# Feed-forward products accumulated in one PSUM bank, activation sums formed with the gate and streamed through DRAM

## The chip, the cores and the metric

The kernel runs on one core of one Trainium2 chip. Its time is the device time of one execution in microseconds (us). Five engines work side by side, each in the order of its own instructions: PE (TensorE, matrix products; its weight loads, PEld, overlap them), DVE (VectorE), ACT (ScalarE), POOL (GpSimd) and SP (which here only issues transfers). They meet through semaphores. DMA engines move data between DRAM and the on-chip memory SBUF. PE writes its products to PSUM, eight banks of 128 x 512 float32 values; DVE and ACT read them there, POOL does not.

## The reference

The program is one layer of a network on 1024 rows of 1024 float32 values: three mixers, a merge with a projection, and a feed-forward. Only the feed-forward is changed:

```python
gu = rms_norm(x, g_ffn[l]) @ w_ffn_in[l]          # 1024 x 1024 by 1024 x 5632
g_, u_ = jnp.split(gu, 2, axis=-1)
x = x + (jax.nn.silu(g_) * u_) @ w_ffn_out[l]     # 1024 x 2816 by 2816 x 1024
```

## The kernel before

**Numbers.** Every float32 operand of a product is split into a high part, which ACT writes (line 105), and a low part, which DVE forms by subtraction (line 106). A product of two split operands is three matmuls (`mm3`, lines 121 to 123): high by high, low by high, high by low. A tile named `fwh` or `foh` is a high part, `fwl` or `fol` a low part.

**Seven products.** Each large product is cut into 2 x 2 blocks and done by the seven block products of Winograd's scheme in place of eight. The operands of the seven are sums of blocks, and the results are sums of products.

**First product.** The width of 5632 columns is worked on in 22 blocks: block j has the same 128 columns of gate and of value (`g_`, `u_`) for all 1024 rows. The tokens' side is kept in SBUF, split, in seven versions: the quarters "11", "21", "22" and the sums "T1" to "T4" (tiles `hh`, `hl`). For each block, `ffn_first` loads half of the block's weights and makes the products with "11" and "21"; `ffn_rest` loads the other half, lets POOL form four weight sums (lines 1153 to 1156), splits them, and makes the five other products. One product (`prod`) is 12 matmuls of 128 x 512 into one bank; banks are taken in turn, eight of them. Each product is read from its bank at once and added into SBUF by DVE (lines 1144, 1162 to 1168). Then comes the gate, by a Tanh on ACT and two operations of DVE for each half of the rows (lines 1180 to 1182); it leaves out a factor of 0.5, which is made up for when the last product is added to x. Activations go to DRAM (`act_dram`), but for those of the last pair of blocks, which stay. `ffn_first` runs two blocks ahead of `ffn_rest`.

**Last product.** The width of 2816 is worked on in 11 pieces of 2 x 128 (`kk`). The sum over the pieces stays in PSUM: two sets of four banks, one bank for each 128 rows of a half of the tokens. There are four steps (`plan`), each over all pieces, with two products a piece, the last with one; a product is four groups of three matmuls. For each piece the step's function (`prep1` to `prep4`) loads weights and activations, forms the sums of either (POOL, marked `G`, and DVE, marked `V`, line 1241), and splits them. This runs `AHEAD = 2` pieces ahead of the products. Activations are loaded once and stay in SBUF until the end. Between steps the banks are added to `xr`, the rows of x, by DVE (line 1352), or copied by ACT and added by POOL (lines 1348 and 1349), and finished quarters are stored.

**Order of the work.** A scheduler with a model of the engines' times reorders the instructions within their dependences when the program is built; the order on each engine is then fixed. `Slots` hands out buffers of 4 KB a partition, the one that has been free longest first. Loads on SP's queue that are marked `keep_in_program_order` stay in the order of the code.

Of the kernel before, what the change touches and what calls it, by code (L numbers as in the profile page):

```python
# [30 lines left out]
AHEAD = 2  # L31
# [8 lines left out]
# Order in which the steps of the independent parts before the merge are emitted.  # L40
# [42 lines left out]
def hybrid_kernel(ctx: ExitStack, tc: tile.TileContext, x, small, cs, bias_a, lru_w, w_idx, w_zg, w_c, w_g, w_b,  # L83
# [129 lines left out]
    # The high parts of a pair of heads in their own halves of e and o, the low parts in the other halves.  # L213
# [10 lines left out]
    # Each part of a pair of heads in both halves, head by head.  # L224
# [14 lines left out]
    # q . k for 128 rows against columns k0 .. k0 + w, with q stacked and each part of k in both halves. Returns the  # L239
    # columns of the two banks.  # L240
# [114 lines left out]
    # Stacked q and k of a pair of heads from the rows of its z (q, q, k, k).  # L355
# [103 lines left out]
    # Softplus of -lambda, from exp(-|z|) by range reduction and log1p by its atanh series.  # L459
# [151 lines left out]
    # Top-k threshold of each row: its bits from the highest down, by counts.  # L611
# [5 lines left out]
    class Chain:  # L617
# [15 lines left out]
        # Go on with the first n tiles.  # L633
# [72 lines left out]
    # The high halves of the scores settle the high bits of the threshold: for these a score reaches a bound if its  # L706
    # high half does.
# [72 lines left out]
    # The sums of the quarters of hT (B11 | B12 over B21 | B22: width by tokens) that the seven products of a 2 x 2  # L780
    # block product (Winograd) take.
# [67 lines left out]
    # The products of a pair of gate columns that take quarters of hT themselves.  # L849
# [83 lines left out]
    # The projection behind the merge goes by the seven products of a 2 x 2 block product (Winograd): rows 512.. are  # L933
    # its first row block, the blocks of M (kp, kp + 2) its columns. P6 and P7 go on top of P1.
# [61 lines left out]
    hb_ = {}  # L996
# [83 lines left out]
    def bank(shape=(128, 512), at=None):  # L1080
        i = nb_[0] % 8 if at is None else at
        nb_[0] += at is None
        return psum.tile(list(shape), F32, name="B", tag=f"B{i}")

# [32 lines left out]
    fw, al, be = {}, {}, {}  # L1117
    act = {(NH - 1, h): None for h in range(2)}
    act_dram = [dram.tile([128, 2, 2, 512], F32, name=f"ad{j}") for j in range(NF // 2)]

    def split_w(raw, n):
        hi, lo = rw.get((128, n, 4, 128), F32R, "fwh"), rw.get((128, n, 4, 128), F32R, "fwl")
        split(raw, hi, lo)
        return hi, lo
# [6 lines left out]
    def prod(w, i, name):  # L1131
        p = bank()
        for k in range(4):
            hi, lo = hb_[name, k // 2]
            mm3(p, w[0][:, i, k], w[1][:, i, k], hi[:, k % 2], lo[:, k % 2], k == 0, k == 3)
        return p

    def ffn_first(j):
        load_a(j)
        al[j] = sl.get((128, 2, 512), F32, "al")  # L1140
        be[j] = sl.get((128, 2, 512), F32, "be")
# [3 lines left out]
        rw.free(*w)  # L1145

    def ffn_rest(j):
# [13 lines left out]
        x, y = al[j], be[j]  # L1161
# [7 lines left out]
        rw.free(*w12, *w34, *w22)  # L1169
        f, kk = j // NH, j % NH  # L1170
        if kk < NH - 1:
            ga = sl.get((128, 2, 512), F32, "act")
            gv = [ga[:, hf] for hf in range(2)]
        else:
            if f == 0:
                for hf in range(2):
                    act[kk, hf] = sl.get((128, 2, 512), F32, "act")
            gv = [act[kk, hf][:, f] for hf in range(2)]
        for hf, (g_, u_) in enumerate(((y[:, 0], x[:, 1]), (x[:, 0], y[:, 1]))):
            S.activation(gv[hf], g_, AF.Tanh, scale=0.5)  # L1180
            V.scalar_tensor_tensor(gv[hf], gv[hf], 1.0, g_, op0=OP.add, op1=OP.mult)
            V.tensor_mul(gv[hf], gv[hf], u_)
        sl.free(x, y)
        if kk < NH - 1:
            nc.gpsimd.dma_start(act_dram[kk][:, :, f], ga)
            sl.free(ga)
# [16 lines left out]
    ring = Slots(arena, fore + rw.free_list + rr.free_list[:4])  # L1203
    sl.free_list = rr.free_list[4:] + sl.free_list
# [3 lines left out]
    order = [0, 1, NH - 1] + list(range(2, NH - 1))  # L1208

    def load_act(n, h):  # L1210
        if n < NH and order[n] != NH - 1:
            kk = order[n]
            act[kk, h] = sl.get((128, 2, 512), F32, "act")
            tc.keep_in_program_order(nc.sync.dma_start(act[kk, h], act_dram[kk][:, h]))

    def load_x(t):
        xt = sl.get((128, D), F32, "xr")
        tc.keep_in_program_order(nc.sync.dma_start(xt, x2_dram[t]))
        xr.append(xt)

    def load_w(kk, q0, q1):
        w = {}
        for q in range(q0, q1, 2):
            n = min(2, q1 - q)
            t = ring.get((128, n, 512), F32, "fo")
            tc.keep_in_program_order(nc.sync.dma_start(t, w_fo[kk, :, q:q + n]))
            for i in range(n):
                w[q + i] = t[:, i]
            w["t", q] = t
        return w  # L1230

    def free_w(w):
        ring.free(*[t for q, t in w.items() if isinstance(q, tuple)])

    def split_into(src, n):
        hi, lo = ring.get((128, n, 512), F32R, "foh"), ring.get((128, n, 512), F32R, "fol")
        for dst, r in src:
            split(r, hi[:, dst], lo[:, dst])
# [195 lines left out]
```

## Time and profile before

| what | us |
|---|---|
| median of 3 runs | 1604.65 |
| lowest and highest run | 1600.42, 1605.0 |
| profiled execution, span from first to last instruction | 1599.2 |
| PE busy, share of the span | 1498.3, 94% |
| DVE, ACT, POOL busy | 1214.5, 742.1, 493.1 |
| first product of the feed-forward, from and to | 903.5, 1335.9 |
| last product, from and to | 1335.9, 1593.8 |

The profiled execution's own time is its span and what lies around it at start and end; the runs without a profile lie 1.2 to 5.8 us above the span. The profile is a single execution. Busy times of the engines overlap. PE's time is shown as busy while matmuls follow each other; its granted clock stands beside it as a share of full speed.

### The profile page before, as it was taken

To read this page: it belongs to the slowest core of one execution; us is meant where nothing else is said; L and a number is where in the kernel's file an instruction comes from. 1 tells how busy PE (TensorE), PEld (TensorE's weight loads), DVE (VectorE), ACT (ScalarE), POOL (GpSimd) and SP (SyncE) were. 2 spreads that over 40 slices of the span, in tenths; PEclk is the share of its full clock that TensorE was granted. 3 is DMA by queue.
4 is the path that set the end of the run, shared out by engine and by line. 5 is a ranking of instruction groups with operands and counts; after the bars stand their busy time and mean duration, and the time that the engine had idled before them with its cause. 6 is when DMAs were issued, how large, how long until landed. Compare 5 with 4: busy or idle time off the path is not lost.

```text
span 1599.2 us, 20503 instructions
## 1 busy us (share of the span) xinstructions
PE 1498.3 (94%) x7612; PEld 1246.1 (78%) x7612; DVE 1214.5 (76%) x2023; ACT 742.1 (46%) x1158; POOL 493.1 (31%) x484
## 2 busy tenths in 40 slices
PE   6999989999999997999989989999999999998886
PEld 5888778988788875888867868888888888876665
DVE  5679999888557679568799897656666566477997
ACT  5456769866788564443123643223222234223332
POOL 1430011210000235540152453333333330385565
PEclk9999999999999999999999999999999999999898
DMA  4011202122111221458441412222222226873432
GB/s 169 27 44 41 79 31 93 54 80 67 55 51 41 80 80 53 142 196 333 159 171 39 145 39 96 91 80 92 80 92 79 79 66 213 277 247 115 156 119 71
DMA packets 49428, 168.73 MB, mean 106 GB/s; under 512 B 5680, under 2 KB 5808, under 8 KB 49328
## 3 DMA queue, kind: packets, MB, share of 16 engines
q1 hardware_dynamic: 37008, 127.31, 23.8%
q0 software_dynamic: 10016, 35.92, 5.9%
q10 hardware_dynamic: 2304, 4.20, 0.7%
q8 instruction: 60, 0.98, 0.2%
q14 instruction: 40, 0.33, 0.1%
HBM read 130.70 MB, written 36.70 MB: 105 GB/s over the span
## 4 chain that ended last, share of the span: by engine, by line
PE 69%; DVE 15%; ACT 4%; issue 4%; DMA 4%; POOL 4%; SPq 0%; DVEq 0%; ACTq 0%; POOLq 0%
PE B L122 12%; PE B L121 12%; PE B L123 12%; PE G L121 7%; PE G L122 7%; PE G L123 7%; DVE key L648 3%; DVE fol L106 2%; PE T L431 2%; DVE ol L106 1%; DMA fo<-in_w_fo 1%; PE T L122 1%; PE T L123 1%; PE T L121 1%; DMA x<-in_x 1%
## 5 line engine op out<-in xcount | busy, mean ns | idle before, releaser
L122 PE MATMUL B<-hl,fwh 128*128 128x512 f32 x616 | 240.5, 391 | 5.3 <-DVE hl L106 5.3
L121 PE MATMUL B<-hh,fwh 128*128 128x512 f32 x616 | 239.8, 390 | 1.8 <-ACT h2r L1019 1.8
L123 PE MATMUL B<-hh,fwl 128*128 128x512 f32 x616 | 239.9, 390 | 0.0
L121 PE MATMUL B<-foh,foh 128*128 128x512 f32 x308 | 119.1, 414 | 26.4 <-ACT foh L105 18.8
L122 PEld LDWEIGHTS B<-hl,fwh 128*128 128x128 f32 x616 | 116.0, 188 | 30.3 <-DVE hl L106 6.4
L121 PEld LDWEIGHTS B<-hh,fwh 128*128 128x128 f32 x616 | 116.2, 189 | 26.2 <-ACT h2r L1019 2.0
L123 PEld LDWEIGHTS B<-hh,fwl 128*128 128x128 f32 x616 | 116.1, 188 | 24.2
L122 PE MATMUL B<-fol,foh 128*128 128x512 f32 x308 | 125.1, 406 | 5.2 <-DVE fol L106 5.1
L123 PE MATMUL B<-foh,fol 128*128 128x512 f32 x308 | 118.0, 399 | 0.0
L122 PE MATMUL G<-wzl,hTh 128*128 128x256 f32 x384 | 110.8, 289 | 4.3 <-DVE wzl L106 4.3
L121 PE MATMUL G<-wzh,hTh 128*128 128x256 f32 x384 | 109.4, 287 | 1.9 <-ACT wzh L105 1.2
L105 ACT ACTIVATE fwh<-s 128x1024 fp32r<-128x1024 f32 x44 | 46.5, 1060 | 137.5 <-PE B L122 131.9
L123 PE MATMUL G<-wzh,hTl 128*128 128x256 f32 x384 | 109.9, 287 | 0.0
L121 PEld LDWEIGHTS B<-foh,foh 128*128 128x128 f32 x308 | 61.2, 199 | 43.7 <-ACT foh L105 21.8
L660 ACT ACTIVATE junk_s<-score,ngS 128x1024 int8<-128x1024 f32 (+2 forms) x78 | 77.6, 995 | 20.9 <-DVE ngS L658 17.0
L1155 POOL TENSOR_TENSOR s<-fa,fb 128x512 f32<-128x512 f32 x22 | 30.5, 1388 | 183.8 <-DVE fwl L106 162.1
L122 PEld LDWEIGHTS G<-wzl,hTh 128*128 128x128 f32 x384 | 74.0, 193 | 5.8 <-DVE wzl L106 4.7
L123 PE MATMUL G<-hTh,wgl 128*128 128x512 f32 x192 | 75.7, 394 | 2.0 <-DVE wgl L106 2.0
L121 PEld LDWEIGHTS G<-wzh,hTh 128*128 128x128 f32 x384 | 73.7, 193 | 3.8 <-ACT wzh L105 1.7
L122 PEld LDWEIGHTS B<-fol,foh 128*128 128x128 f32 x308 | 60.5, 196 | 20.6 <-DVE fol L106 8.0
L121 PE MATMUL G<-hTh,wgh 128*128 128x512 f32 x192 | 76.0, 396 | 0.0
L122 PE MATMUL G<-hTl,wgh 128*128 128x512 f32 x192 | 75.4, 393 | 0.0
(486 smaller groups left out, 4121.2 us busy)
## 6 DMA issues: line engine op xcount, KB each, us to landing
fo<-in_w_fo SPq DMA_DIRECT2D x44, 512.0 KB, 4.6
gl<-gd SPq DMA_DIRECT2D x24, 512.0 KB, 5.5
fa<-in_w_fi SPq DMA_DIRECT2D x22, 512.0 KB, 3.5
fb<-in_w_fi SPq DMA_DIRECT2D x22, 512.0 KB, 3.4
ad<-act POOLq DMA_DIRECT2D x20, 512.0 KB, 3.1
act<-ad SPq DMA_DIRECT2D x20, 512.0 KB, 6.5
ga<-in_w_g SPq DMA_DIRECT2D x18, 512.0 KB, 3.6
x<-in_x SPq DMA_DIRECT2D x12, 512.0 KB, 4.5
```

What stands on the lines that cost most here:

```text
L105: S.activation(hi, raw, AF.Copy)
L106: (eng or V).tensor_tensor(lo, raw, hi.bitcast(F32), op=OP.subtract)
L121: PE.matmul(o, lhsT=lh, rhs=rh, start=first, stop=False, **kw)
L122: PE.matmul(o, lhsT=lh, rhs=rl, start=False, stop=False, **kw)
L123: PE.matmul(o, lhsT=ll, rhs=rh, start=False, stop=last, **kw)
L431: PE.matmul(o[64 * e:64 * e + 64, :], lhsT=v[(b0 + b) // 4][:, (b0 + b) % 4, h, :], rhs=PT[e][:, b, :], start=b == 0, stop=b == nb - 1, sk ...
L648: V.tensor_scalar(o[:, 0:(i + 1) * 128], (keys or score)[i], ap[:, j:j + 1], 0.0, op0=op, op1=OP.add, accum_out=self.cnt[:, j:j + 1])
L660: S.activation(junk_s[:, 0:(i + 1) * 128], score[i], AF.Sign, bias=self.ng.bitcast(F32)[:, j:j + 1], accum_out=self.cnt[:, j:j + 1])
L1155: G.tensor_tensor(s34[:, 0], a[:, 0], b[:, 0], op=OP.subtract)
```

## The change

1. In the first product the results of a block are no longer each added in SBUF. The product "11", then "T2", "T3" and "T4" go onto one bank one after the other, without clearing it; between them ACT or DVE reads the partial sum. "22" goes onto the bank of "T1" in the same way. Three banks in turn serve the first kind (`xbank`), five the others (`ybank`), among them the transposes of the second half of the tokens.
2. The gate is one Silu on ACT, in place of a Tanh on ACT and an operation of DVE. The factor of 0.5 is gone.
3. The activation sums that the last product needs are formed by DVE behind the gate of each second block, and all activations and sums go to DRAM by POOL's queue; every step of the last product loads its own operands again.
4. In the last product the weight sums are formed by DVE, not by POOL and DVE; two of the four weight quarters stay in SBUF from step 2 to step 4. Of the two quarters that take the same banks, DVE adds both; ACT copies the banks before where they are needed at once. POOL has no arithmetic there any more.
5. Preparation runs four pieces ahead. In the last step the last four pieces are worked on bank by bank, so that each bank is added and stored when it is done.

The core of the diff (comments and the unchanged parts of functions left out):

```diff
-AHEAD = 2
+AHEAD = 4
...
+    def ybank(shape=(128, 512)):
+        ny_[0] += 1
+        return bank(shape, 3 + ny_[0] % 5)
...
-            p = bank((128, 4, 128), None if at is None else (at + k) % 4)
+            p = bank((128, 4, 128), (at + k) % 4) if at is not None else ybank((128, 4, 128))
...
+    def xbank():
+        nx_[0] += 1
+        return bank(at=nx_[0] % 3)
...
-        S.activation(al[j][:, 0], prod(w, 0, "11"), AF.Copy)
-        V.tensor_add(be[j][:, 0], al[j][:, 0], prod(w, 1, "21"))
+        xb[j] = prod(w, 0, "11", xbank())
+        S.activation(g[:, 0], xb[j], AF.Copy)
+        V.tensor_add(g[:, 0], g[:, 0], prod(w, 1, "21", ybank()))
...
-        V.tensor_add(x[:, 0], x[:, 0], prod(w12, 1, "T2"))
-        V.tensor_add(x[:, 1], x[:, 0], prod(w34, 0, "T3"))
-        p5 = prod(w12, 0, "T1")
-        V.tensor_add(y[:, 1], x[:, 1], p5)
-        V.tensor_add(x[:, 0], x[:, 0], p5)
-        V.tensor_add(x[:, 0], x[:, 0], prod(w34, 1, "22"))
-        V.tensor_add(x[:, 1], x[:, 1], prod(w22, 0, "T4"))
...
+        prod(w12, 1, "T2", x, False)
+        S.activation(g[:, 1], x, AF.Copy)
+        p5 = prod(w12, 0, "T1", ybank())
+        S.activation(a1, p5, AF.Copy)
+        gate(g[:, 0])
+        prod(w34, 0, "T3", x, False)
+        V.tensor_add(a1, a1, x)
+        prod(w34, 1, "22", p5, False)
+        V.tensor_add(g[:, 1], g[:, 1], p5)
+        gate(g[:, 1])
+        prod(w22, 0, "T4", x, False)
+        V.tensor_mul(a0, g[:, 0], x)
+        V.tensor_mul(a1, a1, g[:, 1])
...
+        nc.gpsimd.dma_start(pair_dram[0][kk], act[0])
+        V.tensor_add(s[:, 0], a21, a22)
+        V.tensor_sub(s[:, 1], s[:, 0], a11)
+        V.tensor_sub(a21, a11, a21)
+        V.tensor_sub(s4[:, kk % 2], a12, s[:, 1])
+        nc.gpsimd.dma_start(pair_dram[1][kk], s)
+        nc.gpsimd.dma_start(pair_dram[2][kk], act[1])
...
+    def gate(t):
+        S.activation(t, t, AF.Silu)
...
+    def prep3(kk):
+        B = weights(kk, 0)
+        a = split_act(2, kk)
         ts = ring.get((128, 2, 512), F32, "T34")
-        TT(G, ts[:, 1], B[2], B[1], SUB)
-        TT(V, ts[:, 1], B[3], ts[:, 1], SUB)
-        TT(V, ts[:, 1], ts[:, 1], B[0], SUB)
-        TT(G, ts[:, 0], B[3], B[2], SUB)
-        TT(V, ss, act[kk, 0][:, 0], act[kk, 1][:, 0], SUB)
+        V.tensor_sub(ts[:, 0], b34[kk][:, 1], b34[kk][:, 0])
+        V.tensor_add(ts[:, 1], ts[:, 0], B[:, 1])
+        V.tensor_sub(ts[:, 1], ts[:, 1], B[:, 0])
...
+            if m == 3 and kk == NH - LATE:
+                for t in range(4):
+                    for n in range(LATE):
+                        if n >= len(ready):
+                            prepare(s + AHEAD + 1 + n - len(ready))
+                        products(ready[n], m, kk + n, b, i, j, t)
+                    after(m, b, t, banks[b][t])
+                continue
```

**The order on PE, in the middle of the first product.** Before: the last three matmuls of "T2" of a block, and the first three of "T3" (a bank is `B` with its number; the token operands 492 and 483 are those of "T2" and "T3").

```order
L121 MATMUL B_9441<-hh_492_8726,fwh_45_9429 128x512
L122 MATMUL B_9441<-hl_493_8727,fwh_45_9429 128x512
L123 MATMUL B_9441<-hh_492_8726,fwl_46_9430 128x512
L121 MATMUL B_9455<-hh_483_8705,fwh_47_9433 128x512
L122 MATMUL B_9455<-hl_484_8706,fwh_47_9433 128x512
L123 MATMUL B_9455<-hh_483_8705,fwl_48_9434 128x512
```

Each product has a bank of its own. After: the last matmul of "T1" (bank `B_9577`), and what follows until the first of "T3", which goes on the bank `B_9383` of "T2".

```order
L123 MATMUL B_9577<-hh_494_8760,fwl_48_9552 128x512
L121 MATMUL B_9640<-hh_460_8357,fwh_52_9635 128x512
L122 MATMUL B_9640<-hl_461_8358,fwh_52_9635 128x512
L121 MATMUL B_9654<-hh_462_8361,fwh_52_9635 128x512
L122 MATMUL B_9654<-hl_463_8362,fwh_52_9635 128x512
L121 MATMUL B_9515<-hh_479_8727,fwh_54_9676 128x512
L122 MATMUL B_9515<-hl_480_8728,fwh_54_9676 128x512
L121 MATMUL B_9700<-hh_483_8735,fwh_54_9676 128x512
L122 MATMUL B_9700<-hl_484_8736,fwh_54_9676 128x512
L123 MATMUL B_9640<-hh_460_8357,fwl_53_9636 128x512
L121 MATMUL B_9640<-hh_460_8357,fwh_52_9635 128x512
L121 MATMUL B_9383<-hh_481_8731,fwh_49_9555 128x512
```

Between "T2" and "T3" there are now the 12 matmuls of "T1" and ten of the two next blocks, in pieces of two.

**The order on DVE, in step 3 of the last product, one piece.** Before (`S3` an activation sum, `T34` weight sums, `fol` low parts):

```order
L1241 TENSOR_TENSOR S3_231_12997<-act_577_11936,act_591_12348 128x512
L1241 TENSOR_TENSOR T34_222_12947<-fo_221_12945,T34_222_12947 128x512
L106 TENSOR_TENSOR fol_227_12959<-S3_223_12952,foh_226_12958 128x512
L1241 TENSOR_TENSOR T34_222_12947<-T34_222_12947,fo_220_12943 128x512
L106 TENSOR_TENSOR fol_227_12959<-act_590_12304,foh_226_12958 128x512
L106 TENSOR_TENSOR fol_225_12955<-T34_222_12947,foh_224_12954 128x1024
```

After:

```order
L1295 TENSOR_TENSOR T34_155_12369<-fw2_568_11897 128x512
L106 TENSOR_TENSOR fol_154_12366<-fa_152_12363,foh_153_12365 128x1024
L1296 TENSOR_TENSOR T34_155_12369<-T34_155_12369,fw_151_12361 128x512
L1297 TENSOR_TENSOR T34_155_12369<-T34_155_12369,fw_151_12361 128x512
L106 TENSOR_TENSOR fol_157_12374<-T34_155_12369,foh_156_12373 128x1024
```

The sum of activations is gone; the weight sums that POOL did (two a piece) stand here; low parts are made in two operations, not three.

**The order on ACT, at the start of the first product.** Before, up to the first copy of a transpose (`h2r`) of the second half of the tokens:

```order
L105 ACTIVATE fwh_7_8758<-s34_5_8749 128x1024
L1143 ACTIVATE al_472_8578<-B_8580 128x512
L105 ACTIVATE fwh_9_8762<-fb_3_8746 128x512
L1143 ACTIVATE al_474_8614<-B_8616 128x512
L105 ACTIVATE fwh_11_8847<-fa_6_8845 128x1024
L1019 ACTIVATE h2r_476_8644<-B_8645,sm_68 128x512
```

After:

```order
L105 ACTIVATE fw_9_8788<-fb_3_8772 128x512
L105 ACTIVATE fwh_10_8864<-fa_6_8862 128x1024
L1159 ACTIVATE gx_473_8641<-B_8642 128x512
L1221 ACT_TABLE_LOAD
L1221 ACTIVATE gx_472_8606<-gx_472_8606 128x512
L105 ACTIVATE fwh_12_8905<-s12_8_8899 128x1024
L1221 ACTIVATE gx_473_8641<-gx_473_8641 128x512
L1023 ACTIVATE h2r_474_8670<-B_8671,sm_68 128x512
```

Ahead of that copy there are now a table load, two gates and the split of a weight sum of the second block.

## Rows read from the trace of the kernel before

**Rows 1.** The page's first line.

```profile
span 1599.2 us, 20503 instructions
```

**Rows 2.** Stretches: us, busy us (instructions) of PE, PEld, DVE, ACT, POOL, clock, DMA share, GB/s.

```profile
903.50:1335.90 432.40, 425.29 (x1882) 351.60 (x1882) 291.38 (x373) 140.11 (x179) 153.36 (x111) 0.99 0.25 84
1000.00:1300.00 300.00, 300.00 (x1325) 248.51 (x1324) 183.53 (x236) 86.91 (x109) 101.96 (x81) 1.00 0.24 82
1335.90:1593.80 257.90, 226.25 (x925) 180.24 (x923) 200.21 (x180) 82.21 (x103) 140.74 (x85) 0.94 0.52 174
```

**Rows 3.** Waits of PE, last product: engine, line, released by: total us, times, longest.

```profile
PE B L121 <- ACT foh L105: 18.8, 7, 6.8
PE B L121 <- DVE xr L1352: 7.6, 3, 5.9
PE B L122 <- DVE fol L106: 5.1, 6, 2.3
```

**Rows 4.** One short stretch of the last product, columns as in rows 2.

```profile
1490.00:1500.00 10.00, 3.33 (x8) 2.66 (x9) 10.00 (x9) 1.65 (x3) 6.84 (x5) 0.61 0.31 106
```

**Rows 5.** Timeline of PE at either clock: start us, us, engine, line, operation.

```profile
1566.02 0.39 PE L122 MATMUL B<-fol,foh 128*128 128x512 f32 x1
...
1470.51 0.63 PE L123 MATMUL B<-foh,fol 128*128 128x512 f32 x1
...
1470.94 0.63 PE L121 MATMUL B<-foh,foh 128*128 128x512 f32 x1
```

**Rows 6.** DVE by line and shape, last product: busy us, mean ns, idle before.

```profile
L106 DVE TENSOR_TENSOR fol<-T,foh 128x1024 fp32r<-128x1024 f32 x22 | 36.4, 1653 | 10.0 <-ACT foh L105 9.8
...
L1241 DVE TENSOR_TENSOR T<-fo,T 128x512 f32<-128x512 f32 x11 | 12.9, 1171 | 2.4 <-POOL T L1241 2.4
```

**Rows 7.** Timeline of DVE: one split, one subtraction beside POOL, one without.

```profile
1342.95 1.22 DVE L106 TENSOR_TENSOR fol<-act,foh 128x1024 fp32r<-128x1024 f32 x1
...
1512.11 1.77 DVE L1241 TENSOR_TENSOR T<-fo,T 128x512 f32<-128x512 f32 x1
...
1515.02 0.68 DVE L1241 TENSOR_TENSOR T<-T,fo 128x512 f32<-128x512 f32 x1
```

**Rows 8.** Timeline of POOL at the same place.

```profile
1511.60 1.74 POOL L1241 TENSOR_TENSOR T<-fo 128x512 f32<-128x512 f32 x1
```

**Rows 9.** Two stretches of the last product's first step, columns as in rows 2.

```profile
1350.00:1400.00 50.00, 50.00 (x222) 41.41 (x221) 25.87 (x24) 17.14 (x17) 14.32 (x10) 1.00 0.84 279
1400.00:1450.00 50.00, 45.48 (x187) 35.55 (x186) 37.93 (x26) 14.52 (x14) 42.64 (x24) 0.97 0.65 223
```

**Rows 10.** Line views of ACT: duration ns min/median/max, first and last start.

```profile
L1143 ACT ACTIVATE al<-B x22: 576/598/602, 908.9 to 1306.1; 128x512 f32<-128x512 f32 x22
...
L1180 ACT ACTIVATE act<-al x22: 613/613/637, 953.3 to 1335.3; 128x512 f32<-128x512 f32 x22
```

**Rows 11.** Timeline at two handovers between engines: start us, us, engine.

```profile
1559.83 0.63 ACT L105 ACTIVATE foh<-S 128x512 fp32r<-128x512 f32 x1 [3.96 <-POOL S L1241]
...
1560.52 0.79 PE L121 MATMUL B<-foh,foh 128*128 128x512 f32 x1 [4.96 <-ACT foh L105]
...
1592.64 1.07 PE L123 MATMUL B<-foh,fol 128*128 128x512 f32 x4
...
1593.06 2.48 DVE L1352 SCALAR_TENSOR_TENSOR xr<-B,xr 128x512 f32<-128x512 f32 x4 [4.12 <-PE B L123]
```

**Rows 12.** Timeline of ACT, POOL and PE at the first product's start.

```profile
914.39 1.06 ACT L105 ACTIVATE fwh<-fa 128x1024 fp32r<-128x1024 f32 x1 [1.89 <-PE B L122]
...
916.26 4.73 ACT L1019 ACTIVATE h2r<-B,sm 128x512 f32<-128x512 f32 x8 [0.81 <-PE B L1018]
...
915.93 2.14 POOL L1154 TENSOR_TENSOR s<-s,fa 128x512 f32<-128x512 f32 x1
...
931.39 0.79 PE L122 MATMUL B<-hl,fwh 128*128 128x512 f32 x1 [5.30 <-DVE hl L106]
```

**Rows 13.** Line view of ACT, the table load of an earlier stage.

```profile
L555 ACT ACT_TABLE_LOAD  x4: 1283/1283/1283, 390.7 to 493.2; - x4
```

More of the change, by code (lines that the diff above doesn't have):

```diff
@@ L1179, in ffn_rest @@
[L1179 to L1186, printed above, removed]
+        f, kk = j // NH, j % NH
+        if f == 0:
+            act[0], act[1] = (sl.get((128, 2, 512), F32, "act") for _ in range(2))
@@ L1221, in load_w @@
[L1221 to L1238, printed above, removed]
-        return hi, lo
@@ new lines, in load_x, with split_act, weights, prep1 @@
+    def load_x(t):
+        xr.append(load(sl.get((128, D), F32, "xr"), x2_dram[t]))
+    def split_act(m, kk):
+        raw = load(ring.get((128, 2, 512), F32, "fa"), pair_dram[m][kk])
+        a = split_pair(raw)
+        ring.free(raw)
+        return a
+    def weights(kk, q):
+        return load(ring.get((128, 2, 512), F32, "fw"), w_fo[kk, :, q:q + 2])
+    def prep1(kk):
+        B = weights(kk, 0)
+        a = split_act(0, kk)
+        if kk > 2:
+            load_x(kk - 3)
+        w = split_pair(B)
+        ring.free(B)
+        return a, w
@@ L1307, in hybrid_kernel @@
[L1307 to L1313 removed]
+        (prep1, ((0, 0, 1), (1, 1, 0))),
+        (prep2, ((0, 1, 1), (1, 0, 0))),
@@ L1314, in hybrid_kernel @@
+        (prep3, ((0, 0, 0), (1, 1, 1))),
+        (prep4, ((1, 0, 0),)),
+    ]
+    steps = [(m, kk) for m in range(4) for kk in range(NH)]
     ready = []
@@ L1317, in prepare, with quad, add_bank, store @@
         if s < len(steps):
-            m, n = steps[s]
-            ready.append(plan[m][0](n, order[n]))
+            m, kk = steps[s]
+            ready.append(plan[m][0](kk))
+    def quad(h, t, c):
+        return xr[4 * h + t][:, 512 * c:512 * c + 512]
+    def add_bank(p, h, t, c, sign=1.0):
+        o = quad(h, t, c)
+        V.scalar_tensor_tensor(o, p, sign, o, op0=OP.mult, op1=OP.add)
+    def store(h, t, c, eng):
+        r = 128 * (4 * h + t)
+        eng.dma_start(out[r:r + 128, 512 * c:512 * c + 512], quad(h, t, c))
+    def after(m, b, t, p):
+        if m == 0:
+            add_bank(p, 0, t, 0)
+            if b == 1:
+                store(0, t, 0, nc.scalar)
+        elif m == 1 and b == 0:
+            add_bank(p, 0, t, 1)
+        elif m == 1:
+            tmp = ring.get((128, 512), F32, "pt")
+            S.activation(tmp, p, AF.Copy)
+            for h in range(2):
+                V.tensor_add(quad(h, t, 1), quad(h, t, 1), tmp)
+            ring.free(tmp)
+        elif m == 2 and b == 1:
+            add_bank(p, 1, t, 0, -1.0)
+        elif m == 2:
+            add_bank(p, 1, t, 0)
+            store(1, t, 0, nc.scalar)
+            add_bank(p, 1, t, 1)
+            store(1, t, 1, nc.scalar)
+        else:
+            add_bank(p, 0, t, 1)
+            store(0, t, 1, nc.sync)
+    def products(ops, m, kk, b, i, j, t):
+        a, w = ops
+        c = slice(128 * t, 128 * t + 128)
+        mm3(banks[b][t], a[0][:, i, c], a[1][:, i, c], w[0][:, j], w[1][:, j], kk == 0 and (b == 1 or m == 0),
+            kk == NH - 1, skip_group_check=True)
     for s in range(AHEAD):
@@ L1355, in hybrid_kernel @@
-    sl.free(*act.values(), *xr)
+            if m == 3 and kk == NH - LATE:
[5 more added lines that the diff above has]
+                    after(m, b, t, banks[b][t])
+                continue
+            for t in range(4):
+                products(ready[0], m, kk, b, i, j, t)
+            if kk == NH - 1:
+                for t in range(4):
+                    after(m, b, t, banks[b][t])
@@ L1356, in hybrid_kernel @@
+        for a, w in (ready if m == 3 and kk == NH - LATE else [ready.pop(0)]):
+            ring.free(*a[2:], *w[2:])
+    sl.free(*xr)
     ps.__exit__(None, None, None)
```

194 lines of the change are left out of this document (77 added, 117 removed).

## The prediction

> **What bounds the kernel now.** The page comes first: one core, a span of 1599.2 us [rows 1], TensorE busy nearly throughout. An average over a program of unlike stages settles nothing, so the next view is the busy time by stretch [rows 2]. There the reader sees two different halves of the feed-forward. From 1000 to 1300 us, inside its first product, PE is busy 300.0 of 300.0 us at a granted clock of 1.00 and issues 1325 matmuls: 300 / 1325 = 0.2264 us each, the price of one 128x512 matmul at full speed. From 1335.9 us on the last product runs until its last matmul ends at about 1593.8 us: 257.9 us for 4 steps over 11 pieces of the width, (24 + 24 + 24 + 12) x 11 = 924 matmuls. At 0.2264 us these are 209.2 us, so this stage loses 257.9 - 209.2 = 48.7 us. No work on another engine can win more than that, bar the few microseconds at both ends.
>
> Where the 48.7 us go is in the waits of PE in this stage [rows 3]: 18.8 + 7.6 + 5.1 = 31.5 us, all for operands that ACT and DVE had not split yet, or for banks that DVE had not emptied. The remaining 17.2 us are clock: behind a wait the granted clock falls (0.61 in the stretch from 1490 us, where PE is busy 3.3 of 10 us and DVE all 10 [rows 4]). Then a matmul takes 0.63 us and the next starts 0.43 us later, against 0.39 us [rows 5] and the 0.2264 us above; these are the levels of 1.2 and 2.4 GHz. So DVE is what PE waits for, directly or through ACT, which waits for sums.
>
> Why DVE is late: its operations are longer than they need be. In the last product the split of a 128x1024 weight sum takes 1653 ns in the mean and a 128x512 subtraction 1171 ns [rows 6]. The timeline has the same shapes at 1.22 and 0.68 us while POOL stands still, and the subtraction at 1.77 us while POOL runs its own [rows 7, 8]. POOL is busy 140.7 us in this stage [rows 2].
>
> **The change, part by part.** *Last product.* POOL loses all its arithmetic there. Activation sums (33 on POOL, 33 on DVE) leave the stage; the weight sums move to DVE (2 per piece in step 2, 3 in step 3), and of the bank sums that POOL added to the second of two quarters DVE now takes both. With POOL still I price DVE at 1.22 us per 128x1024 and 0.68 us per 128x512. Step 1: two splits, 2.44 us. Step 2: 2 x 0.68 + 2 x 1.22 = 3.80 us. Step 3: 3 x 0.68 + 2 x 1.22 = 4.48 us. Step 4: 2 x 0.68 = 1.36 us. PE needs 24 x 0.2264 = 5.43 us in the first three and 2.72 us in the last. Over the stage DVE has 66 x 1.22 + 22 x 0.68 + 55 x 0.68 + 36 x 0.68 (bank additions) = 157 us against PE's 209 us. DVE is under PE in every step, and preparation now runs 4 steps ahead instead of 2, so a late load or a burst of bank additions (12 x 0.68 = 8.2 us at the tightest boundary) falls into 4 x 5.43 us of cover. If that cover were gone, the 7.6 us of bank waits would stay as they are. Bounds of what is left of the 48.7 us: nothing, or 17.5 us if DVE stays as slow as it is (second rival). I leave 4 us for the three boundaries and the ramp, half of the 7.6 us that they cost today: the gain is 44.7 us, and late next is nothing but PE itself.
>
> *DMA.* The first step loads 11 weight pieces, 11 activation pieces and 8 rows of x, 30 x 0.524 MB in 59.8 us: 263 GB/s. The trace has 279 GB/s at a DMA share of 0.84 with PE at full speed [rows 9]. Steps 2 and 3 ask for 1.31 and 1.05 MB per 5.43 us, 241 and 193 GB/s. Hidden, unless loads start late. SP's queue is kept in program order, and every load of the next pieces stands behind one that waits for a slot; the first slots come from the retired 11 and 21 operands, two blocks before the end of the first product, so the queue is not held then. The extra writes (39 on POOL's queue instead of 20) lie in the first product, at 84 GB/s now.
>
> *First product.* PE is full there, so no relief of DVE (11 half-width operations a block become 7) can win anything; the question is what the new arrangement may lose. Products of a block now go onto one of three banks in turn, and each must wait until the engine that reads the bank between them is done: T3 for the copy of T2's sum, T4 for DVE's addition, and the product "22" for the copy of P5's bank. One eviction takes 0.60 us [rows 10]. From the last matmul of a bank to the next on it I work out 0.16 (the rest of a 0.39 us matmul behind its 0.23 us slot) + 0.03 (last matmul of the first bank, 1592.64 + 0.39, to the addition at 1593.06) + 0.60 + 0.06 (ACT's end at 1560.46 to PE at 1560.52) = 0.85 us [rows 10, 11]. The order now puts other products between: behind T2 come T1 (12 matmuls) and 10 more, 22 x 0.2264 = 5.0 us of cover for 0.85 us. ACT gets two more copies a block, 1.2 us in 19.0 us, and is busy 140.1 of 432.4 us [rows 2]. What stands in line behind a waiting copy on ACT are splits for later blocks, whose slots free in the same order. So I cost the piling at nothing; if the cover were missing it is the slower case below.
>
> I know one rule that speaks against it. The Trainium skill, PSUM — Partial Sum Buffer, section "PSUM bank collisions raise a hardware error", says that two engines may not be on one bank at once, and that readers and writers must be kept apart bank by bank. By it every one of these handovers is a real wait, none may overlap; the trace has such a wait where no other bank had work, DVE's bank additions of the last product, the longest 5.9 us [rows 3]. It prices no wait; the price above is from rows.
>
> *Start of the first product.* Here something is lost. ACT's first copy of the second token half's transposes started at 916.26 us, 0.8 us after its previous work (914.39 + 1.06); DVE's chain of sums and splits follows that copy, and PE stood 5.3 us for one of them until 931.39 us [rows 12]. Now ACT has a table load (1.28 us, [rows 13]), two Silu (about 0.63 us, as the Tanh that they replace, [rows 10]) and a weight split (1.06 us) ahead of that copy: 3.6 us, and the split waits for a POOL sum that ended at 918.07 us (915.93 + 2.14) [rows 12]. The chain shifts by some 3.5 us; PE gets one more split operand to work on meanwhile. I take +3 us. Bounds: -3 us (a shorter chain to the first operand, as T1 is split before the second pair of sums) and +8 us (the shift, and the low clock of that wait as much longer).
>
> *End.* The last four pieces of the last step go bank by bank, so at the end one addition stands behind the last matmul, not four in a row (0.60 us from start to start, 2.48 us for four) [rows 11]: -1.8 us. The store behind it stays.
>
> **Sum.** 1599.2 + 3 - 44.7 - 1.8 = 1555.7 us, a change of -43.5 us. The profiled span is 1.2 us under the lowest run shown and 5.4 us under the median of 1604.65 us, so the median becomes 1604.65 - 43.5 = 1561 us.
>
> **Rivals.** (1) *Bank handovers, slower.* Should PE in fact stand at each of the 3 handovers of a block, because ACT or DVE are behind their static order by the length of the cover, then 22 x 3 x 0.85 = 56 us are added: 1561 + 56 = 1617 us. It is slower than before from 43.5 / 66 = 0.66 us per handover on. For it: three banks where eight rotated, and in-order queues. Against it: the order's 20 and more matmuls between them, and ACT two thirds idle. (2) *DVE stays slow for another reason than POOL.* With 1.65 and 1.17 us, step 2 costs 5.64 us and step 3 costs 6.81 us against 5.43 us: (0.21 + 1.38) x 11 = 17.5 us, 1578 us. For it: the means of [rows 6] hold over a whole stage; against it: the short ones beside an idle POOL. (3) *Loads bound the first step.* If only the 223 GB/s of the next 50 us were to be had [rows 9], 15.7 MB take 70.5 instead of 59.8 us: 1572 us. Against it: 279 GB/s just before that. (4) *The gain is taken back*, by partial handover waits or a starved start of the last product of about 44 us together: no change, 1604 us.
>
> **How the numbers follow.** The forecast gets 0.70, with a range of its own of 1551 to 1571 us (nothing lost at boundaries and start, or both at their upper bounds). Rival (1) 0.07, (2) 0.09, (3) 0.06, (4) 0.05; 0.03 remain for a mishap on either side. Less than 0.3% (4.8 us) can't be told from no change. Faster: 0.70 + 0.09 + 0.06 + 0.02 = 0.87; same 0.05; slower 0.08. The range runs from 1551 us past (3) and (2) with a part of a mishap on top: 1590 us.
>
> **What would show it.** Right: in the last product PE's waits under 6 us, a granted clock of 1.00, about 212 us for it; no POOL arithmetic there; 128x1024 splits at 1.22 us and 128x512 at 0.68 us in all steps. In the first product 0.2264 us per matmul as before. At its start a wait for an operand split near 931 us, some 3 us longer or later. Wrong: waits of PE for copies of x's bank or of P5's bank in the first product (rival 1); splits above 1.5 us with POOL idle (rival 2); ACT waiting for the loads of weights or activations in the first step (rival 3).

## The result, and the profile after

The changed kernel takes 1559.48 us (median of 4 runs, 1559.07 to 1560.7) against 1602.54 us (1599.33 to 1605.0) for the kernel before, run beside it: a ratio of 0.9732, 95% interval 0.9714 to 0.975, 43 us faster. 1561 us was forecast. The profiled span is 1557.9 us, 41.3 us under that of before [rows 1].

The stretches first, with the columns of [rows 2]: the two products, the middle of the first, and the two stretches that answer to [rows 9].

```profile
904.40:1338.00 433.60, 422.69 (x1861) 348.25 (x1861) 259.38 (x280) 161.61 (x221) 155.85 (x126) 0.99 0.30 100
1000.00:1300.00 300.00, 300.00 (x1325) 248.43 (x1324) 167.78 (x175) 102.44 (x142) 104.20 (x93) 1.00 0.31 104
1350.00:1400.00 50.00, 49.11 (x215) 39.96 (x214) 28.46 (x28) 22.79 (x23) 0.55 (x1) 1.00 1.00 385
1400.00:1450.00 50.00, 50.00 (x222) 41.44 (x221) 43.25 (x52) 20.87 (x21) 0.00 (x0) 1.00 0.77 258
1338.00:1553.90 215.90, 214.95 (x946) 177.00 (x944) 147.38 (x183) 79.20 (x89) 2.15 (x4) 1.00 0.62 223
```

The reader is to see three things. The last product takes 215.9 us in place of 257.9 us (its edge to the first product is soft: 25 matmuls of the first product still run after 1338 us, a few of its own before), at a granted clock of 1.00. The middle of the first product is what it was, 1325 matmuls in 300.0 us, with DVE at 167.78 us in place of 183.53 us. And POOL does nothing but issue four transfers in the last product.

Then the waits of PE, in the last product (two lines) and, behind the dots, in the first; columns as in [rows 3].

```profile
PE B L122 <- DVE fol L106: 0.4, 1, 0.4
PE B L121 <- ACT foh L105: 0.4, 1, 0.4
...
PE B L122 <- DVE hl L106: 8.7, 3, 3.6
PE B L121 <- ACT h2r L1023: 1.6, 1, 1.6
```

31.5 us of waits have become 0.8 us in the last product; in the first, 7.1 us (1.8 + 5.3, all at its start) have become 10.3 us, all at its start too, and two short ones of 0.3 us each. DVE's groups in the last product, by line and shape with their mean, answer to [rows 6]:

```profile
L106 DVE TENSOR_TENSOR fol<-fa,foh 128x1024 fp32r<-128x1024 f32 x31 | 37.8, 1221 | 5.6 <-ACT foh L105 5.1
L106 DVE TENSOR_TENSOR fol<-T,foh 128x1024 fp32r<-128x1024 f32 x22 | 26.7, 1218 | 2.6 <-ACT foh L105 2.6
L1335 DVE SCALAR_TENSOR_TENSOR xr<-B,xr 128x512 f32<-128x512 f32 x28 | 18.1, 682 | 27.2 <-PE B L123 27.2
L1286 DVE TENSOR_TENSOR T<-fw,T 128x512 f32<-128x512 f32 x11 | 7.4, 684 | 0.1
```

1653 ns have become 1218 ns, 1171 ns have become 684 ns: every split and sum has the length that only those beside an idle POOL had before. The end of the timeline answers to the last rows of [rows 11]:

```profile
1553.45 0.39 PE L123 MATMUL B<-fo,fo 128*128 128x512 f32 x1
1553.88 0.69 DVE L1335 SCALAR_TENSOR_TENSOR xr<-B,xr 128x512 f32<-128x512 f32 x1 [2.03 <-PE B L123]
```

One addition stands behind the last matmul, not four; from that matmul's end (1553.84 us) to the end of the span there are 4.1 us, before there were 5.4 us.

### The profile page after: what moved, and what is told of

It reads as the page before. It is cut to its first block, busy times and chain, and to the rows that moved or that the text cites. A ratio compares the mean times of both kernels' runs of the same rounds, so it can differ in the third digit from the quotient of the medians.

```text
span 1557.9 us, 20304 instructions
## 1 busy us (share of the span) xinstructions
PE 1485.1 (95%) x7612; PEld 1239.6 (80%) x7612; DVE 1128.8 (72%) x1932; ACT 760.5 (49%) x1188; POOL 356.6 (23%) x418
## 5 line engine op out<-in xcount | busy, mean ns | idle before, releaser
L122 PE MATMUL B<-hl,fwh 128*128 128x512 f32 x528 | 207.1, 393 | 8.7 <-DVE hl L106 8.7
L121 PE MATMUL B<-hh,fwh 128*128 128x512 f32 x528 | 203.0, 391 | 1.6 <-ACT h2r L1023 1.6
L123 PE MATMUL B<-hh,fwl 128*128 128x512 f32 x528 | 199.7, 392 | 0.3 <-DVE fwl L106 0.3
L122 PEld LDWEIGHTS B<-hl,fwh 128*128 128x128 f32 x528 | 99.9, 189 | 30.7 <-DVE hl L106 10.0
L121 PEld LDWEIGHTS B<-hh,fwh 128*128 128x128 f32 x528 | 99.8, 189 | 22.7 <-ACT h2r L1023 1.8
L123 PEld LDWEIGHTS B<-hh,fwl 128*128 128x128 f32 x528 | 99.8, 189 | 21.2 <-DVE fwl L106 0.5
L122 PE MATMUL B<-fol,foh 128*128 128x512 f32 x264 | 102.8, 390 | 0.4 <-DVE fol L106 0.4
L121 PE MATMUL B<-foh,foh 128*128 128x512 f32 x264 | 101.1, 390 | 0.4 <-ACT foh L105 0.4
L106 DVE TENSOR_TENSOR fwl<-s,fwh 128x1024 fp32r<-128x1024 f32 x44 | 53.8, 1224 | 63.0 <-PE B L122 60.5
L123 PEld LDWEIGHTS G<-wzh,hTl 128*128 128x128 f32 x384 | 74.3, 193 | 0.4 <-issue 0.2
```

The costliest lines, as they stand in the source:

```text
L106: (eng or V).tensor_tensor(lo, raw, hi.bitcast(F32), op=OP.subtract)
L121: PE.matmul(o, lhsT=lh, rhs=rh, start=first, stop=False, **kw)
L122: PE.matmul(o, lhsT=lh, rhs=rl, start=False, stop=False, **kw)
L123: PE.matmul(o, lhsT=ll, rhs=rh, start=False, stop=last, **kw)
```

## The experiments

Theory A is the prediction's: POOL beside DVE made DVE late in the last product, everything else costs or wins a few microseconds. Against it stand B (the gain comes from preparing earlier, or from loading instead of summing activations) and C (DVE has too many operations, whoever runs beside it, so that the work could not have been moved to it alone). All ratios below are to the kernel before, which ran beside each with medians of 1601.19 to 1602.54 us.

**The kernel before, without POOL in the last product.** POOL's 85 operations there (eight lines of the code) go to DVE, and nothing else:

```diff
-        TT(G, ts[:, 0], B[2], B[1], SUB)
-        TT(G, ts[:, 1], B[3], ts[:, 0], SUB)
+        TT(V, ts[:, 0], B[2], B[1], SUB)
+        TT(V, ts[:, 1], B[3], ts[:, 0], SUB)
...
-                        G.tensor_tensor(o, o, tmp, op=OP.add)
+                        V.tensor_tensor(o, o, tmp, op=OP.add)
```

> The kernel before, with POOL's 77 sums and 8 additions of the last product moved to DVE and nothing else. Theory A: DVE gets more operations, 85 x 0.68 = 58 us, but all of its operations fall to 0.68 and 1.22 us; step 2 then needs 5.16, step 3 5.98 and step 4 3.4 us against PE's 5.43, 5.43 and 2.72 us, (0.55 + 0.68) x 11 = 13.5 us over, so of the 48.7 us some 31 are won: about 1571 us, with POOL idle there. Theory C (DVE has too many operations, whoever runs beside it): with durations as they are, 85 x 1.17 = 99 us come on top of 200 us in a stage of 258 us: 1640 us and more.

1564.99 us, ratio 0.9778 (0.9759 to 0.9796): 36 us below the kernel before that ran beside it (1601.19 us), of the 43 us of the change. The expected 1571 us was 6 us too high. Its last product as one stretch, PE's waits in it, and the weight splits on DVE:

```profile
1339.30:1560.50 221.20, 212.74 (x921) 174.55 (x921) 188.70 (x263) 82.59 (x103) 0.00 (x0) 0.98 0.60 202
...
PE B L121 <- ACT foh L105: 8.5, 3, 4.7
...
L106 DVE TENSOR_TENSOR fol<-T,foh 128x1024 fp32r<-128x1024 f32 x22 | 26.8, 1217 | 0.0
```

DVE does 263 operations here, before 180, and is busy less: 188.70 us against 200.21 us [rows 2]. Work was added to the late engine, and it became earlier. C is refuted, and it is shown that POOL's arithmetic in the last product is what cost most of the time. In which way it did so, this run does not tell, for it takes away two things at once: the long operations of DVE, and the sums that POOL itself made late. In the kernel before, ACT's splits waited longer for sums of POOL than for sums of DVE (`S` activation sums, `T` weight sums; columns as in [rows 3]):

```profile
ACT foh L105 <- POOL S L1241: 24.5, 10, 5.2
ACT foh L105 <- POOL T L1241: 19.7, 7, 4.9
ACT foh L105 <- DVE S L1241: 15.4, 6, 4.4
ACT foh L105 <- DVE T L1241: 14.6, 3, 6.6
```

Of the seven waits of PE for a high part, 18.8 us, five with 11.7 us end behind a sum that POOL finished last; the longest of the five stands in [rows 11]. No run gives the two ways their shares.

The stage still loses 221.2 - 921 x 0.2264 = 12.7 us here, near the 13.5 us that were expected, and 1.7 us in the changed kernel. So the other edits, the activation sums that stream through DRAM and the deeper preparation among them, win some 11 us more in the last product, of which the changed kernel's start takes back 6 us (worked out below).

**The change with two pieces of preparation in place of four.**

```diff
-AHEAD = 4
+AHEAD = 2
...
-        prepare(s + AHEAD)
         if m == 3 and kk > NH - LATE:
             continue
+        prepare(s + AHEAD)
```

(The call moves because with two pieces the last four, which are worked on together, prepare theirs themselves.)

> The changed kernel, but preparing 2 pieces ahead as before, not 4. Theory A (the gain is DVE's time in the last product, since POOL's arithmetic beside it is gone): DVE still needs 2.4 to 4.5 us where PE needs 5.43 us, so only the cover at the three boundaries gets thinner (12 bank additions, 8.2 us, against 2 x 5.43 us): 1560 to 1568 us. Theory B (the deeper preparation is what hides the waits): most of the 43 us comes back, above 1590 us.

1564.75 us, ratio 0.9771 (0.975 to 0.9792), in A's range. PE has one wait of 3.1 us for a split of the last product, in its first step at 1367.9 us, where it had 0.4 us; at the three boundaries it does not wait. The depth is worth some 5 us. The second half of B, loading in place of summing activations, no run tries by itself.

**The kernel before with three pieces in place of two.**

```diff
-AHEAD = 2
+AHEAD = 3
```

> The kernel before, preparing 3 pieces ahead instead of 2 (its buffers allow no more); POOL keeps its sums. Theory A (DVE's time, long because POOL runs beside it): in step 3 DVE needs 1.18 + 1.17 + 0.87 + 1.65 + 1.11 + 1.08 = 7.1 us by its own means against PE's 5.43 us, so a deeper start only shifts the wait: 1592 to 1603 us. Theory B (depth): 1580 us or less.

1613.89 us, ratio 1.0078 (1.0064 to 1.0092): slower by 12 us, and so outside what either theory expected. PE's waits in the last product, and a weight sum on DVE:

```profile
PE B L121 <- ACT foh L105: 30.9, 8, 13.4
PE B L121 <- DVE xr L1352: 11.7, 4, 9.8
...
L1241 DVE TENSOR_TENSOR T<-fo,T 128x512 f32<-128x512 f32 x11 | 18.7, 1702 | 24.1 <-POOL T L1241 24.1
L106 DVE TENSOR_TENSOR fol<-T,foh 128x1024 fp32r<-128x1024 f32 x22 | 28.0, 1274 | 5.8 <-ACT foh L105 5.8
```

DVE stands 24.1 us for POOL's part of a weight sum (2.4 us before [rows 6]), while its weight splits are shorter than before (1274 ns against 1653 ns). By the means of this run its six operations of a piece of step 3 take 0.71 + 1.70 + 0.87 + 1.27 + 0.94 + 0.68 = 6.2 us in place of 7.1 us, and yet the kernel is slower. So it is not DVE's time alone here, but a chain of engines, POOL to DVE to ACT to DVE, that sets a piece's time. That one more piece of depth wins nothing here is shown; why it makes the chain slower stays open.

**The change with the weight sums of steps 2 and 3 back on POOL**, two for each piece:

```diff
-        V.tensor_sub(ts[:, 0], b34[kk][:, 0], B)
-        V.tensor_sub(ts[:, 1], b34[kk][:, 1], ts[:, 0])
+        G.tensor_tensor(ts[:, 0], b34[kk][:, 0], B, op=OP.subtract)
+        G.tensor_tensor(ts[:, 1], b34[kk][:, 1], ts[:, 0], op=OP.subtract)
```

> The changed kernel, with two weight sums of every piece in steps 2 and 3 given back to POOL (44 operations). Theory A in its exact form (what counts is DVE's time for a piece, not that POOL runs): splits beside POOL grow towards 1.65 us, but DVE has 2 x 1.65 = 3.3 us in step 2 and 1.2 + 3.3 = 4.5 us in step 3 against 5.43 us, so PE hardly waits: 1558 to 1566 us, with long DVE operations in the trace. Theory A' (any POOL work beside DVE costs): the waits come back, 1575 us or more.

1560.21 us, ratio 0.9737 (0.9724 to 0.975): no change. Yet DVE is as slow again as before:

```profile
L106 DVE TENSOR_TENSOR fol<-T,foh 128x1024 fp32r<-128x1024 f32 x22 | 38.3, 1743 | 7.5 <-ACT foh L105 7.1
L1335 DVE SCALAR_TENSOR_TENSOR xr<-B,xr 128x512 f32<-128x512 f32 x28 | 17.8, 682 | 26.1 <-PE B L123 26.1
L1297 DVE TENSOR_TENSOR T<-T,fw 128x512 f32<-128x512 f32 x11 | 14.1, 1280 | 0.0
L1352 DVE TENSOR_TENSOR xr<-xr,pt 128x512 f32<-128x512 f32 x8 | 8.4, 1092 | 0.0
...
PE B L122 <- DVE fol L106: 0.5, 1, 0.5
PE B L121 <- ACT foh L105: 0.2, 1, 0.2
```

This sharpens A. Long DVE operations cost nothing by themselves: a piece of step 3 now has 1.74 + 1.57 (a split of activations at its mean) + 1.28 = 4.59 us of DVE, still under PE's 5.43 us. In step 3 of the kernel before, a piece's sum passed PE's time: its six operations, by their means in the last product, take 1.18 (activation sum) + 1.17 + 0.87 (weight sums) + 1.11 + 1.08 (two half-size splits of activations) + 1.65 = 7.06 us. Here are its steps 2 to 4, each from its first matmul on (columns as in [rows 2]):

```profile
1395.70:1469.52 73.82, 63.39 (x265) 50.07 (x264) 57.54 (x47) 22.01 (x23) 53.29 (x30) 0.97 0.55 188
1469.52:1547.11 77.59, 66.93 (x264) 52.95 (x265) 71.69 (x70) 26.11 (x37) 44.65 (x27) 0.90 0.40 134
1547.11:1593.71 46.60, 36.13 (x132) 27.69 (x132) 39.70 (x36) 12.68 (x21) 32.45 (x21) 0.89 0.26 89
```

Against 264, 264 and 132 matmuls at 0.2264 us they lose 14.1, 17.8 and 16.7 us; step 1 loses nothing. Step 3 fits the sum: 11 x (7.06 - 5.43) = 17.9 us. Step 2 does not: its three operations take 1.27 + 1.68 + 1.65 = 4.6 us, as much as a piece of the run above, which loses nothing with four pieces of preparation. 5.9 of its 14.1 us are the wait for banks at its end [rows 3]; of its other five waits three end behind single splits of 2.2 to 2.3 us. In step 4 DVE's 1.27 + 1.11 + 1.33 = 3.7 us a piece pass PE's 2.72 us, but all of its 10.5 us of waits end behind a sum of POOL's. So the sum per piece fits one step of three. How much POOL's own lateness adds in the others is read from waits, not tried: POOL's sums and two pieces of preparation were not run together in the changed kernel.

The rows also show which operations suffer: the addition from a bank (`B`, one operand in SBUF) keeps its 682 ns, the same shape with both operands in SBUF takes 1092 ns. The Trainium skill, SBUF — State Buffer, section "Who interferes with whom", says that a DVE instruction with two SBUF inputs contends with a GpSimd instruction that reads SBUF, and that one with at most one SBUF input, outside the modes that use both ports, does not. The trace agrees: in the kernel before, 9 of the 28 additions from a bank ran wholly beside an operation of POOL and took 678 ns in the mean.

**The change without covers for the handovers.** To price the slower rival, PE's products of a block are held in the order T2, T3, T4, T1, "22" (`keep_in_program_order`), so that each follows directly on its bank (the order of matmuls within a product changes with it, and which of T1 and T3 is copied):

```diff
+                tc.keep_in_program_order(x_)
...
-        p5 = prod(w12, 0, "T1", ybank())
...
         prod(w34, 0, "T3", x, False)
+        S.activation(a1, x, AF.Copy)
+        prod(w22, 0, "T4", x, False)
+        p5 = prod(w12, 0, "T1", ybank())
```

> The changed kernel, with PE held to the order T2, T3, T4, T1, 22, 11, 21 in each block, so that each of the three handovers of a bank (T2 to T3, T3 to T4, T1 to 22) has no other product in front of it. This prices rival 1 of the prediction. By the price worked out there, 0.85 us each: 66 x 0.85 = 56 us more, about 1615 us, and some us more at the start of the first product, where PE can't take other work either. If a handover costs nothing (other engines read and PE writes at once): 1560 us.

1713.08 us, ratio 1.0708 (1.0683 to 1.0733), beyond what was expected. PE's waits in the first product, and its middle:

```profile
PE B L1148 <- ACT gx L1189: 44.9, 20, 4.2
PE B L1148 <- DVE act L1194: 36.6, 21, 2.1
PE B L1148 <- ACT act L1191: 15.2, 21, 1.0
...
1000.00:1400.00 400.00, 325.47 (x1320) 252.30 (x1319) 169.70 (x170) 106.86 (x141) 105.80 (x88) 0.97 0.22 75
```

62 waits, three a block less a few, of 96.7 / 62 = 1.56 us. The mildest kind has 15.2 / 21 = 0.72 us, near the 0.85 us that was worked out (of which 0.16 us is the last matmul itself). The others are longer where the reader's queue is not free. One of 4.16 us ended at 1101.05 us with this on ACT, and behind the dots on PE:

```profile
1099.89 0.63 ACT L1227 ACTIVATE gx<-gx 128x512 f32<-128x512 f32 x1 [4.55 <-DVE gx L1166]
1100.42 0.58 ACT L1189 ACTIVATE gx<-B 128x512 f32<-128x512 f32 x1
...
1101.05 0.50 PE L1148 MATMUL B<-hh,fwh 128*128 128x512 f32 x1 [4.16 <-ACT gx L1189]
...
1102.16 0.63 PE L1149 MATMUL B<-hl,fwh 128*128 128x512 f32 x1
1102.59 0.63 PE L1150 MATMUL B<-hh,fwl 128*128 128x512 f32 x1
```

The copy that frees the bank (second line) stood behind a gate that had itself waited 4.55 us for DVE. Besides the 75 us of waits in 400 us, PE is busy 27 us longer than the 298.9 us that 1320 matmuls need at 0.2264. Some 11 us of it are the clock: 54 matmuls start 0.43 us apart, as the last two rows do (the level of 1.2 GHz). The rest lies mostly at the waits: 47 of the 62 fall into this stretch, each with the 0.16 us of the last matmul before it and a slower first one behind it. A bare handover thus costs (400 - 298.9) / 47 = 2.15 us here, not 0.85 us; over the whole run, where the start loses more too, it is 154 / 66 = 2.3 us. The price of the rival was too low; it is the order, with 20 and more matmuls between, that keeps the rival away.

**The change with a bank of its own for each product**, eight in turn, added up by DVE in SBUF:

```diff
-        return bank(shape, 3 + ny_[0] % 5)
+        return bank(shape, ny_[0] % 8)
...
-        prod(w12, 1, "T2", x, False)
-        S.activation(g[:, 1], x, AF.Copy)
+        V.tensor_add(g[:, 1], g[:, 1], prod(w12, 1, "T2", ybank()))
+        V.tensor_add(a0, g[:, 1], prod(w34, 0, "T3", ybank()))
...
```

> The changed kernel, but in the first product every product again has a bank of its own (eight in turn) and DVE adds it in SBUF; Silu, the activation sums and the last product stay as changed. Theory A: PE is full in the first product either way, so the piling is worth nothing: 1557 to 1563 us. Rival D (piling relieves DVE and that gives part of the gain): 4 more additions a block, 22 x 4 x 0.68 = 60 us more of DVE, and a time of 1570 us or more.

1555.99 us, ratio 0.9714 (0.9699 to 0.9729), 3.5 us below the change, with overlapping intervals, and 1 us below what was expected: piling up in one bank wins nothing. The middle, from 1000 to 1300 us, again has 1325 matmuls in 300.0 us, though DVE is busy 207.9 us there in place of 167.8 us. PE waits 7.9 us at the start in place of 10.3 us, and by the line views it does 135 matmuls of products from 904.4 to 950 us in place of 116. So the piling costs some 4 us at the start (19 x 0.2264 = 4.3 us in the one profile of each). Own banks win this although ACT's first copy of a transpose starts no earlier than in the change, at 920.22 us, and two of DVE's splits take 3.4 us each, as in the kernel before (behind the dots):

```profile
920.22 0.67 ACT L1023 ACTIVATE h2r<-B,sm 128x512 f32<-128x512 f32 x1
931.17 6.75 DVE L106 TENSOR_TENSOR hl<-h2r,hh 128x1024 fp32r<-128x1024 f32 x2
...
927.96 6.69 DVE L106 TENSOR_TENSOR hl<-h2r,hh 128x1024 fp32r<-128x1024 f32 x2
```

**Two edits at the start of the first product.** One has the four 128x1024 subtractions of POOL among the token sums on DVE (one of the two lines is shown), the other puts the transposes of the second half of the tokens ahead of the first two blocks, as before:

```diff
-            G.tensor_tensor(b12, b22, b12, op=OP.subtract)
+            V.tensor_sub(b12, b22, b12)
...
+    trans2_second(xn, raws2)
...
-    trans2_second(xn, raws2)
```

> The changed kernel, with the four 128x1024 subtractions that POOL makes at the start of the first product moved to DVE. Theory A applied to the other place where PE waits: there DVE's 14 operations run at 2 to 3.4 us while POOL works. Eighteen at 1.14 us from start to start are 20.5 us, against some 25 us now: 3 to 5 us less, about 1555 us. Rival: DVE is full there, four more operations make PE wait longer: 1562 us or more.

> The changed kernel, with the transposes and operand sums of the second half of the tokens put ahead of the first two blocks' first products in the program's text, so that ACT's copies no longer stand behind the table load, two Silu and a weight split. If these 3.6 us on ACT are why PE waits longer at the start than before: 3 to 6 us less, 1554 to 1557 us. If DVE's chain alone sets it: 1559 us.

1557.8 us, ratio 0.972 (0.9705 to 0.9735), and 1558.15 us, ratio 0.9724 (0.9711 to 0.9738): neither can be told from the change. The runs of the first lie apart, two at 1553.11 and 1553.41 us, three from 1557.8 to 1559.02 us, and the profiled one is that of 1553.11 us. Its timeline shows the mechanism again. In the change, POOL's subtraction and DVE's split beside it; behind the dots the same split with POOL's work on DVE:

```profile
932.33 3.38 POOL L1046 TENSOR_TENSOR h2r<-h2r,h2r 128x1024 f32<-128x1024 f32 x1 [2.36 <-DVE h2r L1045]
933.42 3.37 DVE L106 TENSOR_TENSOR hl<-t,hh 128x1024 fp32r<-128x1024 f32 x1
...
928.22 1.22 DVE L106 TENSOR_TENSOR hl<-t,hh 128x1024 fp32r<-128x1024 f32 x1
```

3.37 us against 1.22 us for one split; the last split of the tokens starts at 939.0 us, in the change at 945.7 us, though DVE does four operations more. Of these 6.7 us, 2.8 us are not the edit's: the first product began at 901.6 us in this execution, in the change at 904.4 us. From its first matmul to 950 us PE did 145 matmuls of products and lost 950 - 901.6 - 145 x 0.2264 = 15.6 us, in the change 950 - 904.44 - 116 x 0.2264 = 19.3 us. A wait for ACT (2.8 us, for a high part) comes next there. Why three of five runs show next to no gain stays open.

**Both together**: own banks, and the start's subtractions on DVE; and the same with the transposes ahead.

> The changed kernel with a bank of its own for every product of the first product (as in the run with own banks, 1555.99 us against 1559.48) and the four 128x1024 subtractions of POOL at the start on DVE (as in the run with that edit, 1557.8 against about 1559.5). Theory A (the two losses are separate: pieces of PE's wait at bank handovers, and a DVE chain at the start that POOL's reads slow): the gains add, 1559.5 - 3.5 - 1.7 = 1554 us, range 1551 to 1557; PE's waits between 920 and 945 us under 7 us together. Rival B (both gains come out of the same waits at the start): 1556 us, no better than own banks alone.

> The same, and the second token half's transposes put ahead of the first two sets of pieces of the next operand, so ACT's copies of the transposes come before its two Silu and its weight split, as the kernel before had it. Theory A (DVE's chain sets the start, and it is short now, so that ACT's copies are next in line): about 1 us less than without this edit, 1553 us. Rival B (the first T1 operand, split later, is what PE wants): 1 us or more above the run without it.

1551.95 us (1549.97 to 1552.62), ratio 0.9683 (0.967 to 0.9697), and 1552.8 us, ratio 0.9694 (0.9681 to 0.9707). The first is the fastest kernel of this study, 7.5 us below the change, inside the range of its theory A, with an interval apart from that of either edit alone. The order of the transposes makes no difference that can be told. The start, in the change and then with both edits:

```profile
920.00:950.00 30.00, 19.36 (x75) 14.33 (x74) 26.59 (x16) 18.82 (x25) 15.18 (x6) 0.89 0.06 18
...
920.00:950.00 30.00, 27.42 (x110) 22.48 (x111) 28.77 (x27) 17.15 (x22) 4.27 (x3) 0.89 0.10 35
```

Counted by the line views from 904.4 to 950 us and without the 32 short transposes, PE does 153 matmuls in place of 116: 37 x 0.2264 = 8.4 us, as much as the difference of the spans (1549.5 against 1557.9 us), though this execution also began the first product 1.5 us earlier. Counted as above, from the first matmul on, the start loses 11.3 us (158 matmuls from 902.91 us on) in place of 19.3 us. With own banks alone it loses 14.7 us (135 from 904.69 us on), with the subtractions alone 15.6 us: 4.6 and 3.7 us less, 8.3 us together, against 8.0 us with both. So the gains add, and both edits pay at the start: a short DVE chain, and free banks in which PE may work on other products meanwhile. That the banks are what held PE is argued from this stretch alone; the scheduler's order changed with them, and the two were not tried apart.

## Why the prediction was right, step by step

The sum of terms, from the two profiled executions. PE's two products hold 1848 + 924 = 2772 matmuls, 627.6 us at 0.2264. Before they took 690.3 us (903.5 to 1593.8), 62.7 us over; now 649.4 us (904.4 to 1553.84), 21.8 us over.

- *Last product, 44.7 us expected.* Of the 21.8 us, 0.9 us of idle and some 0.8 us of slower matmuls lie in the last product (215.84 us for 946 matmuls, 214.2 us at 0.2264). 48.7 - 1.7 = 47.0 us were won. Nothing was left for the boundaries, where I had left 4 us, and nothing with two pieces of preparation either: the 3.1 us that came back then lie in the first step.
- *The cause, POOL beside DVE.* Right that POOL's arithmetic costs the time: taking it away in the kernel before won 36 us. Right that it makes DVE's operations long; the second rival, that DVE stays slow without POOL, is refuted by 128x1024 splits at 1218 to 1224 ns. The prediction names DVE alone as what PE waits for, directly or through ACT. It overlooked that POOL was late itself: ACT's wait of 3.96 us in [rows 11] was for a sum of POOL's, and such sums end 11.7 of the 18.8 us of PE's waits for high parts. It also gave all of 17.2 us to the clock, where 51 matmuls started 0.43 us apart, some 10 us; the rest lies around the waits. Neither touches the sum, since the change removes DVE's long operations and POOL's sums together.
- *DMA.* Right that it stays hidden, but for another reason than the one given: the first step's loads did not spread over 59.8 us at 263 GB/s, they ran in front at 385 GB/s from 1350 to 1400 us (279 in [rows 9]), and PE stood 0.9 us.
- *First product, piling, 0.* Right for the middle: 300.0 us for 1325 matmuls in both kernels. At the start it was not nothing (next point). That the order's cover is what makes it free is shown by taking it away, which cost 154 us, where the rival had 56 us.
- *Start, +3 us.* Mis-sized: 21.8 - 1.7 = 20.1 us are lost there, before 432.4 - 1848 x 0.2264 = 14.0 us, so +6.1 us, within the bounds of -3 and +8 us; the matmuls of products from 904.4 to 950 us say the same, 116 against 143, 27 x 0.2264 = 6.1 us. The shift was seen: ACT's first copy of a transpose started at 920.59 in place of 916.26 us [rows 12], behind the table load and a split that waited 3.42 us for POOL. What I priced as one shift was three waits of 2.2 to 3.6 us behind DVE's splits, some of which ran at 3.4 us beside POOL's subtractions. I had read that very effect in the last product and did not look for it here. But it is not what was added: the kernel before has DVE operations of 3.2 to 3.4 us beside POOL at this place too. With own banks the copy starts as late and two splits still take 3.4 us each, and yet 19 of the 27 matmuls come back. So the larger part of the 6.1 us is the piling, which I had priced at nothing; whether it is the fewer banks or the order that the scheduler makes of them is not shown.
- *Tail, -1.8 us.* -1.3 us.

Together with 0.9 us by which the first product began later (not explained): +0.9 + 6.1 - 47.0 - 1.3 = -41.3 us, the difference of the spans. The forecast of -43.5 us is that close because two errors of opposite sign, 2.3 us too little in the last product and 3 us too little loss at the start, met: that it is so close is in part luck. The feature that the title names first, products that pile up in one bank, is no part of the gain.

## What to carry to other kernels

Where an engine is late, compare its operations' means with the shortest of the same shape in the trace, and see what ran beside the long ones: moving a neighbour's work onto the late engine can make it early. Then compare the sum per piece with the time of the engine that waits, and follow each wait back to the engine that ended it: here the neighbour was late itself, and the sum fitted one step of three. A bank that is read between two products needs other work for PE as long as the reader's queue, not as long as the read.

## What was not expected of the hardware

- A 128x1024 subtraction with both operands in SBUF took DVE 3.37 us beside one of POOL of 3.38 us, against 1.22 us alone: 2.8 times, more than the 1653 ns against 1218 ns that the last product's means show.
- Transfers, almost all loads of 4 KB rows, ran at 385 GB/s over 50 us, with ten microseconds of them at 416 GB/s in the row below, and PE was hardly held:

```profile
1360.00:1370.00 10.00, 9.11 (x39) 6.86 (x38) 6.72 (x6) 5.08 (x5) 0.00 (x0) 1.00 1.03 416
```

- Preparing one piece earlier made the kernel before 12 us slower, under 1% but clear of the noise (ratio 1.0064 to 1.0092); the cause is open.
